# Hybrid stick-breaking / RWKV-7 step on one core: the builder's clock books an in-place operation with its own input, and an eviction nearer to its matmul

## The chip, the cores and the metric

The program runs on one core of a Trainium2 chip. The metric is the device time of one execution in microseconds. Before and after are each the median of several executions; one further execution is recorded by the hardware profiler, and all rows below come from it.

## The reference

One layer of a streaming encoder, for 512 prompt tokens and 8 running streams of 16 tokens (640 tokens, width 1024, 16 heads of 64 in each branch):

```python
h = _rmsnorm(x, norm_g)
proj = jnp.einsum('btd,dc->btc', h, w_in)            # one projection, 10368 columns
# branch A: stick-breaking attention, strictly causal
log_keep = jnp.where(valid, jax.nn.log_sigmoid(-z), 0.0)
later = lax.cumsum(log_keep, axis=3, reverse=True) - log_keep
weight = jnp.where(valid, jnp.exp(jax.nn.log_sigmoid(z) + later), 0.0)
y_a = jnp.einsum('btc,cd->btd', o_a * jax.nn.silu(z_a), w_o_a)
# branch B: RWKV-7, per head a 64x64 state
S = S * w_t - (S kk_t) (kk_t * a_t)^T + v_t k_t^T     # written short
o_t = S r_t
y_b = jnp.einsum('btc,cd->btd', o_b * jax.nn.silu(z_b), w_o_b)
y = jnp.einsum('btd,de->bte', g_a * y_a + g_b * y_b, w_out)
return x + y, k, v, shift_new, wkv_new
```

The final states of the 8 sampled streams (`wkv_sample`) and of the prompt (`wkv_prompt`) are outputs too.

## The kernel before

**Tiling.** Everything is transposed: features lie on the 128 partitions, the 640 tokens on the free axis. A projection job (`gemm_range`) makes 128 output columns for 640 tokens, in two halves of 320. Weights and inputs are each split into a high and a low part, so that for each of 8 slices of the contraction there are three matmuls: `ps_g<-xh,whi`, `ps_g<-xl,whi` and `ps_g<-xh,wlo`, 48 a job. They are the bulk of TensorE's work. After every second slice (six matmuls, below called a piece) the job gives the builder a chance to place something else.

**Stages.** First the norm (up to about 40 us). Then, to about 720 us, the RWKV branch for eight pairs of heads, with projections between. Then a stretch of projections, then attention for eight pairs (about 796 to 1030 us), again with projections between; at last the two branch projections, the merge and the output projection.

**RWKV, per pair of heads.** `prep` makes decay and keys (`wl`, the low part of the two decay and gate matrices, on GpSimd), the operands `H` and `BK` and the masked products `AB`. `prep2` inverts blocks of them through `STG` and `Y`. `chain` walks the chunks of 64 tokens; a step (`step`) goes TensorE `X,H`, ScalarE `RH`, TensorE `RH,AB`, ScalarE `X`, TensorE `X,BKt`, VectorE `X`, and every hand-over passes an engine. `sstate` makes the final states of the sampled streams: GpSimd masks `X` into `ux`, TensorE multiplies it with `BKt` into `psn`, then come three operations in a row:

```python
vtt(sn, psn.rearrange("p (b v) -> p b v", b=8), S0T, ALU.add)
...
gtt(sn, sn, wc[:, 8:16].unsqueeze(2).broadcast_to([128, 8, 64]), ALU.mult)
yield [sn]
```

`vtt` is VectorE, `gtt` is GpSimd, in place; then TensorE transposes `sn` four times. `post` norms and gates the output of a pair; its last part is on GpSimd (`on<-on,V`, `zb<-zb,on`, `zb<-zb,Oa`).

**Attention, per pair.** A sampled block (`KT,qbd`) and eight prompt blocks are each scored on TensorE, pass ScalarE (`kp`, `bt`), GpSimd (`bt<-bt,amsk`) and VectorE (a scan of `kp`, then `bt<-bt,kp`), are transposed on TensorE (`ps_b<-cst,bt`, the flip) and multiplied with the values; `sg` is the gate of the pair's output. `reload("oB")` brings the RWKV branch's output back from memory and splits it over the projections' input tiles: GpSimd copies `xh<-rl`, VectorE makes `xl<-rl,xh`.

**What sets the order.** Each engine runs its instructions in the order in which the program was written, and that order is found while the program is built. The branches are generators, which the `Driver` steps. A `yield [tiles]` says that the stream should go on when these tiles are ready by the builder's clock (`Clock`), an account with one running time for each engine. `Driver.run` compares that with TensorE's time in the account: of the streams that are ready it takes the one of the first priority, and if none is ready it writes a piece of the projection. So what an operation is booked at decides how many projection pieces are written between a hand-over's two ends. `Clock.note` (L138 to L145) books an operation: it starts no sooner than its engine is free and its inputs are ready, and an input that the same engine made counts as ready sooner by `near` (0.25 for TensorE, 0.15 ScalarE, 0.14 VectorE, 0.15 GpSimd), since a result is booked `LAT = 0.25` after its operation's end. `_Eng.__getattr__` (L212 to L217) wraps every instruction: it sorts the operands into inputs and output and calls `note`. All instructions pass its line L213, so rows of the profile are told apart by tile names.

Of the kernel before, what the change touches and what calls it, by code (L numbers as in the profile page):

```python
# [88 lines left out]
class Clock:  # L89
# [46 lines left out]
    def note(self, eng, dur, ins, outs, lat=0.0):  # L136
        st = self.free[eng]
        for i in ins:  # L138
            r = self.ready.get(i)
            if r is not None:  # L140
                st = max(st, r - (self.near[eng] if self.by.get(i) == eng else 0.0))
            if i.startswith("ps_") and self.last.get(i, eng) != eng:
                st = max(st, self.used[i] - 0.12)
        for o in outs:
            st = max(st, self.used.get(o, 0.0) - (self.near[eng] if self.last.get(o) == eng else 0.0))  # L145
        self.free[eng] = st + dur
        if eng == "dma":
            self.wire = max(self.wire, st + dur + lat[1]) + lat[0]
            lat = self.wire + lat[2] - st - dur
        for o in outs:  # L150
            self.ready[o] = st + dur + lat
            self.by[o] = eng
        for o in ins:
            end = st + dur + (lat if eng == "dma" else self.LAT)
            if end > self.used.get(o, 0.0):
                self.used[o], self.last[o] = end, eng
# [5 lines left out]
def _name(ap):  # L162

    if not hasattr(ap, "tensor"):
        return ap
    n = ap.tensor.name
    return f"{n}:{ap.offset % (8 * T) // T}" if n in PARTS else n


def _cols(ap):  # L170
    n = 1
    for d in ap.shape[1:]:
        n *= d
    return n
# [30 lines left out]
class _Eng:  # L205
# [3 lines left out]
    def __getattr__(self, op):  # L209
        f = getattr(self.obj, op)  # L210

        def call(*a, **k):  # L212
            r = f(*a, **k)  # L213
            aps = [x for x in list(a) + list(k.values()) if hasattr(x, "tensor")]
            out = k.get("out", aps[0])
            ins = [x for x in aps if x is not out]
            n = _cols(out)  # L217
            e = self.eng
            lat = Clock.LAT
            if e == "pe":  # L220
                w = k.get("lhsT")
                m, r = (128, 128) if w is None else (_cols(w), w.shape[0])
                if w is None:
                    d = 0.109
                elif w.dtype == F32R:
                    d = max(0.013 + n / 2400.0, 0.107)
                elif w.dtype == F32:
                    d = max(0.026 + n * 0.00087, 0.082 if m > 32 else 0.041) if m <= 64 else \
                        max(n / 600.0 + 0.005, 0.216)
                else:  # L230
                    d = 0.089
                mode = "full" if r > 64 and m > 64 else (r > 32, r > 64, m > 32, m > 64)
                if mode != self.clk.mode:
                    d += 0.1 if self.clk.mode == "full" else 0.2
                    self.clk.mode = mode
            elif e == "act":
                d = 0.065 + n * 0.00085 + 0.1 * sum(hasattr(k.get(x), "tensor") for x in ("scale", "bias"))
                if out.shape[0] < 64:
                    d = 0.12 + n * 0.0021
                elif out.shape[0] < 128:  # L240
                    d += 0.115
                fn = str(k.get("func"))
                t = "sig" if "Sigmoid" in fn or "Tanh" in fn else "exp" if "Exp" in fn else \
                    "sqrt" if "Sqrt" in fn else None
                if t is not None and t != self.clk.tbl:
                    self.clk.tbl = t
                    d += 1.28
            elif e == "dve":
                d = 0.075 + n * 0.00106
                if op == "scalar_tensor_tensor":  # L250
                    d = 0.13 + n * 0.00112
                elif op == "tensor_scalar":
                    d = 0.1 + n * 0.0011 + 0.03 * sum(hasattr(x, "tensor") and _cols(x) == 1
                                                     for x in list(a) + list(k.values()))
                elif op == "tensor_tensor_scan":
                    d = 0.03 + n * 0.0025
                elif op == "reciprocal":
                    d = 0.05 + n * 0.0064
                elif op == "bn_stats":
                    d = 0.126  # L260
                elif op == "transpose" and len(ins[0].shape) > 2 and ins[0].ap[-1][0] > 1:
                    d = 2.03
                if out.shape[0] < 128 and any(_name(x).startswith("ps_") for x in ins if hasattr(x, "tensor")):
                    d += 0.09
            elif e == "pool":
                d = 0.2 + n * (0.0022 if op == "tensor_tensor" else 0.0012)
                if op == "tensor_copy":
                    d = 0.15 + n * 0.0035
            else:
                d = 0.47  # L270
                run = 2.0 if min(x.shape[-1] for x in aps) < 128 else 1.0
                lat = (n * out.shape[0] * 4 * run / 3.6e5, 0.65, 0.93)
            self.clk.note(e, d, [_name(x) for x in ins], [_name(out)], lat)
            return r
        return call
# [1504 lines left out]
```

## Time and profile before

| | us |
|---|---|
| three executions | 1175.71, 1171.71, 1172.51 |
| median | 1172.51 |
| the profiled execution, its own time | 1171.08 |
| span of its trace | 1169.3 |
| TensorE busy (matmul) | 1111.5 |
| VectorE busy | 746.2 |
| ScalarE busy | 629.8 |
| GpSimd busy | 390.5 |

Busy is the time in which at least one instruction of the engine ran. TensorE is busy for 95% of the span, so that 57.8 us are left in which it waits. Its clock can be lower than full (2.4 GHz) in places: the column PEclk of a stretch is the granted share, 0.50 being the level of 1.2 GHz.

### The profile page before, as it was taken

The numbers are of one execution on the slowest core, as the hardware profiler recorded it, in microseconds if no ns is written. First come the engines' busy times: TensorE is split into PE (matmuls) and PEld (weight loads), VectorE is DVE, ScalarE is ACT, GpSimd is POOL, SyncE is SP. The second block draws the span as 40 slices with busy tenths as digits, with TensorE's granted clock in tenths as the row PEclk, the third lists the DMA queues.
The fourth block names the chain that finished last, engine by engine and source line by source line (L and its number), as shares of the span: only waits on it lengthen the run. The fifth ranks groups of instructions, "written<-read, shape, count | busy, mean of one in ns | idle before, by whom it ended". The sixth has DMA issues, their size and how long they took to land. (4 is left out here: it accounts for less than half of the span.)

```text
span 1169.3 us, 25426 instructions
## 1 busy us (share of the span) xinstructions
PE 1111.5 (95%) x10050; PEld 1037.7 (89%) x10050; DVE 746.2 (64%) x1517; ACT 629.8 (54%) x1347; POOL 390.5 (33%) x605
## 2 busy tenths in 40 slices
PE   6999899989999999999899999999999989999997
PEld 4989899979989989889799899998888878899997
DVE  6485974847765867857767544337777688765424
ACT  5636357646666477466575556445555544522223
POOL 3033315125222243342342513034444454323302
PEclk9999999989999999999999999999999999999999
DMA  5222222213132232133132333369666676366312
GB/s 193 78 89 57 78 66 82 84 50 115 62 95 77 67 93 79 55 88 89 52 93 90 98 103 102 108 184 261 180 161 160 172 216 177 82 197 188 105 56 91
DMA packets 205294, 130.70 MB, mean 112 GB/s; under 512 B 78332, under 2 KB 184696, under 8 KB 205176
## 3 DMA queue, kind: packets, MB, share of 16 engines
q1 hardware_dynamic: 204888, 129.03, 37.8%
q8 instruction: 79, 1.29, 0.4%
q14 instruction: 39, 0.32, 0.1%
q0 software_dynamic: 288, 0.05, 0.0%
HBM read 97.70 MB, written 31.35 MB: 110 GB/s over the span
## 5 line engine op out<-in xcount | busy, mean ns | idle before, releaser
L213 PE MATMUL ps_g<-xh,whi 128*128 128x320 f32 (+1 forms) x1424 | 468.5, 329 | 1.7 <-ACT xh L213 1.3
L213 PE MATMUL ps_g<-xl,whi 128*128 128x320 f32 (+1 forms) x1424 | 443.5, 311 | 3.3 <-DVE xl L213 3.3
L213 PE MATMUL ps_g<-xh,wlo 128*128 128x320 f32 (+1 forms) x1424 | 443.0, 311 | 1.4 <-DVE wlo L213 1.4
L213 PEld LDWEIGHTS ps_g<-xh,whi 128*128 128x128 f32 x1424 | 271.4, 191 | 9.3 <-issue 3.0
L213 PEld LDWEIGHTS ps_g<-xl,whi 128*128 128x128 f32 x1424 | 270.9, 190 | 6.4 <-DVE xl L213 4.5
L213 PEld LDWEIGHTS ps_g<-xh,wlo 128*128 128x128 f32 x1424 | 270.0, 190 | 2.4 <-DVE wlo L213 2.4
L213 DVE TENSOR_TENSOR wlo<-raw,whi 128x1024 fp32r<-128x1024 f32 x97 | 123.6, 1274 | 69.6 <-ACT whi L213 69.0
L213 ACT ACTIVATE whi<-raw 128x1024 fp32r<-128x1024 f32 x97 | 102.7, 1059 | 48.6 <-DMA raw<-in_w_o_a_dram 28.6
L213 DVE TENSOR_TENSOR_SCAN kp<-kp,amsk 128x256 f32<-128x256 f32 (+3 forms) x80 | 73.6, 929 | 27.8 <-ACT kp L213 27.7
L213 POOL TENSOR_TENSOR bt<-bt,amsk 128x128 f32<-128x128 f32 x64 | 44.0, 691 | 124.3 <-ACT bt L213 81.5
L213 POOL TENSOR_TENSOR itmp<-INV 128x28 f32<-128x28 f32 (+6 forms) x112 | 47.0, 420 | 90.8 <-DVE INV L213 82.9
L213 ACT ACTIVATE kp<-ps_a 128x512 f32<-128x512 f32 (+3 forms) x72 | 33.1, 460 | 68.0 <-PE ps_a L213 42.2
L213 ACT ACTIVATE RH<-ps_b 128x128 f32<-128x128 f32 (+1 forms) x64 | 19.4, 302 | 77.8 <-PE ps_b L213 77.4
L213 ACT ACTIVATE sp<-ps_g 128x320 f32<-128x320 f32 x80 | 34.6, 437 | 45.9 <-PE ps_g L213 40.6
L213 ACT ACT_TABLE_LOAD x39 | 50.0, 1283 | 8.9 <-DVE BK L213 5.4
L213 DVE SCALAR_TENSOR_TENSOR X<-ps_b,wc,SW 64x64 f32<-64x64 f32 x96 | 26.7, 278 | 35.7 <-PE ps_b L213 34.9
L213 POOL TENSOR_TENSOR on<-on,V 128x640 f32<-128x640 f32 x8 | 12.4, 1550 | 108.9 <-ACT on L213 108.9
L213 DVE TENSOR_TENSOR bt<-bt,kp 128x511 f32<-128x511 f32 (+4 forms) x72 | 42.4, 588 | 7.7 <-POOL bt L213 0.3
L213 POOL TENSOR_TENSOR INV<-INV,itmp 128x28 f32<-128x28 f32 (+6 forms) x112 | 43.6, 390 | 8.8
L213 PE MATMUL ps_b<-cst,bt 128*128 128x128 f32 x192 | 33.5, 278 | 12.4 <-DVE bt L213 11.8
L213 PE MATMUL ps_g<-olo,mgh 128*128 128x256 f32 x160 | 45.0, 281 | 0.0
L213 PE MATMUL ps_g<-ohi,mgh 128*128 128x256 f32 x160 | 45.0, 281 | 0.0
(252 smaller groups left out, 2319.4 us busy)
## 6 DMA issues: line engine op xcount, KB each, us to landing
raw<-in_w_in_dram SPq DMA_DIRECT2D x81, 512.0 KB
q<-dr_q SPq DMA_DIRECT2D x32, 160.0 KB
Kr<-in_cache_sb_k_dram SPq DMA_DIRECT2D x16, 256.0 KB
Vp<-in_cache_sb_v_dram SPq DMA_DIRECT2D x16, 256.0 KB
raw<-in_w_o_b_dram SPq DMA_DIRECT2D x8, 512.0 KB
raw<-in_w_o_a_dram SPq DMA_DIRECT2D x8, 512.0 KB
oraw<-in_w_out_dram SPq DMA_DIRECT2D x4, 1024.0 KB
dr_zB<-zm SPq DMA_DIRECT2D x8, 320.0 KB
```

Of the source, the lines that this page charges most:

```text
L213: r = f(*a, **k)
```

## The change

Two edits of the builder's clock; no instruction of the kernel is written, removed or sized anew.

```diff
@@ -138,7 +138,8 @@
         for i in ins:
             r = self.ready.get(i)
             if r is not None:
-                st = max(st, r - (self.near[eng] if self.by.get(i) == eng else 0.0))
+                by = self.by.get(i)
+                st = max(st, r - (self.near[eng] if by == eng else 0.12 if by == "pe" else 0.0))
             if i.startswith("ps_") and self.last.get(i, eng) != eng:
                 st = max(st, self.used[i] - 0.12)
         for o in outs:
@@ -213,7 +214,7 @@
             r = f(*a, **k)
             aps = [x for x in list(a) + list(k.values()) if hasattr(x, "tensor")]
             out = k.get("out", aps[0])
-            ins = [x for x in aps if x is not out]
+            ins = [x for k, x in enumerate(aps) if x is not out or any(x is y for y in aps[:k])]
             n = _cols(out)
             e = self.eng
             lat = Clock.LAT
```

The first edit: an operation on another engine that reads a result of TensorE is booked 0.12 us sooner. The second: an operand that is the very object given as the output was left out of the inputs before; now its second appearance counts as an input, so that an in-place operation is booked behind the operation that made its operand. It bears on `sn`, on `sg` of attention, on `newton` and on some more.

Both programs hold the same instructions, as many on each engine; their order differs from TensorE's 408th row on, and is the same again in the last 997 rows (the output projection). The helper's line is L214 now, since a line was added above it.

TensorE, the seventh pair's (pair 6) sampled state, from the matmuls on `ux` to the four transposes of `sn` (`ps_g` are projection matmuls, `X,BKt`, `X,AB` and `X,H` are of the chain's steps, `cst,V` and `H,BK` are of `prep`). Before:

```order
L213 MATMUL ps_g<-xh,wlo 128x320
L213 MATMUL ps_b<-X,BKt 128x128
L213 MATMUL ps_c<-X,AB_102 128x128
L213 MATMUL ps_a<-cst,V 128x128 x5
L213 MATMUL ps_g<-xh,whi 128x320
L213 MATMUL ps_g<-xl,whi 128x320
L213 MATMUL ps_g<-xh,wlo 128x320
L213 MATMUL ps_g<-xh,whi 128x320
L213 MATMUL ps_g<-xl,whi 128x320
L213 MATMUL ps_g<-xh,wlo 128x320
L213 MATMUL ps_b<-ux,BKt 64x256 x2
L213 MATMUL ps_b<-cst,sn 128x128 x4
```

The same place now:

```order
L214 MATMUL ps_g<-xh,wlo 128x320
L214 MATMUL ps_b<-ux,BKt 64x256 x2
L214 MATMUL ps_a<-H,BK 128x128 x4
L214 MATMUL ps_g<-xh,whi 128x320
L214 MATMUL ps_g<-xl,whi 128x320
L214 MATMUL ps_g<-xh,wlo 128x320
L214 MATMUL ps_g<-xh,whi 128x320
L214 MATMUL ps_g<-xl,whi 128x320
L214 MATMUL ps_g<-xh,wlo 128x320
L214 MATMUL ps_b<-X,H 128x128
L214 MATMUL ps_c<-X,H 128x128
L214 MATMUL ps_b<-cst,sn 128x128 x4
```

A piece of the projection and some matmuls of `prep` and of the chain now stand between `ux,BKt` and the transposes, where nothing stood.

VectorE, the first pair's `prep2`, from the tile `Y` to `STG` (`H`, `BK` of `prep`; `K`, `shf` are evictions of the projection). Before:

```order
L213 TENSOR_SCALAR Y_1422<-ps_a,half 128x128
L213 TENSOR_TENSOR K<-K,nrm 128x640
L213 SCALAR_TENSOR_TENSOR H<-kkn,E_1176 64x8x64
L213 SCALAR_TENSOR_TENSOR H<-kkn,E_1176 64x2x64
L213 TENSOR_TENSOR BK<-av,sg 64x10x64
L213 TENSOR_TENSOR BK<-K,sg 64x10x64
L213 COPY AB_102<-ps_a 16x8x16 x2
L213 SCALAR_TENSOR_TENSOR STG<-STG,half,ps_a 32x16x8 x2
```

The same place now:

```order
L214 TENSOR_SCALAR Y_1457<-ps_a,half 128x128
L214 SCALAR_TENSOR_TENSOR kkn<-R,prm,K 128x640
L214 SCALAR_TENSOR_TENSOR K<-ps_g,prm,K 128x192
L214 SCALAR_TENSOR_TENSOR K<-ps_g,prm,K 128x8x15
L214 SCALAR_TENSOR_TENSOR K<-ssft,prm,K 128x8
L214 COPY shf<-ps_g 128x9
L214 COPY AB_102<-ps_a 16x8x16 x2
L214 SCALAR_TENSOR_TENSOR STG<-STG,half,ps_a 32x16x8 x2
```

The next pair's `H` and `BK` stood between `Y` and `STG`; they have moved ahead of `Y`, and one long operation and four evictions stand there.

VectorE, the reload of the RWKV output in attention (`xl<-rl,xh`; `kp` and `bt` are the scan and the product of a score block, `ktok`, `ql` and `ks` belong to the next pair's operands). Before:

```order
L213 TENSOR_TENSOR xl<-rl,xh 128x640 x2
L213 COPY ktok<-ps_b 128x512
L213 TENSOR_TENSOR xl<-rl,xh 128x640 x2
L213 TENSOR_TENSOR sg<-ps_c,sg 128x512
L213 COPY ktok<-ps_b 128x128
L213 TENSOR_TENSOR xl<-rl,xh 128x640
L213 TENSOR_TENSOR wlo<-raw,whi 128x1024
L213 TENSOR_TENSOR xl<-rl,xh 128x640 x3
L213 SCALAR_TENSOR_TENSOR kp<-kp,amsk 128x256 x2
L213 TENSOR_TENSOR bt<-bt,kp 128x2x255
```

The same place now:

```order
L214 TENSOR_TENSOR xl<-rl,xh 128x640
L214 SCALAR_TENSOR_TENSOR kp<-kp,amsk 128x256
L214 TENSOR_TENSOR bt<-bt,kp 128x255
L214 TENSOR_TENSOR xl<-rl,xh 128x640
L214 SCALAR_TENSOR_TENSOR kp<-kp,amsk 128x128
L214 TENSOR_TENSOR bt<-bt,kp 128x127
L214 TENSOR_TENSOR ql<-q_11829,qh 128x512 x2
L214 TENSOR_TENSOR xl<-rl,xh 128x640
L214 TENSOR_TENSOR wlo<-raw,whi 128x1024
L214 TENSOR_TENSOR xl<-rl,xh 128x640 x3
```

The reload stood between two pairs' score blocks, behind the last scan of one pair; now its parts lie between a pair's scans.

Counted over TensorE's whole order, 96 projection matmuls fewer stand ahead of the first pair's `KT,qbd` (3381, 3477 before), and 90 of these ahead of the last RWKV pair's output `Oa`. From one pair's `KT,qbd` to the next, and at last to the last flip, there stand 84, 84, 84, 84, 84, 84, 72 and 60, where there stood 84, 84, 96, 96, 96, 90, 78 and 60. Behind the last flip there are 144 more.

## Rows read from the trace of the kernel before

**Rows 1.** The page's first part: the span, busy time by engine.

```profile
span 1169.3 us, 25426 instructions
...
PE 1111.5 (95%) x10050; PEld 1037.7 (89%) x10050; DVE 746.2 (64%) x1517; ACT 629.8 (54%) x1347; POOL 390.5 (33%) x605
```

**Rows 2.** Windows by stage: busy of each engine (instructions), clock, DMA share, GB/s.

```profile
core 0: us, PE busy (x) PEld busy (x) DVE busy (x) ACT busy (x) POOL busy (x), PEclk, DMA share, GB/s
...
40.00:720.00 680.00, 654.28 (x6392) 615.43 (x6392) 457.86 (x1032) 407.45 (x864) 221.43 (x398) 0.99 0.27 80
720.00:800.00 80.00, 80.00 (x575) 78.86 (x575) 26.20 (x66) 39.03 (x86) 15.13 (x14) 1.00 0.58 161
800.00:1040.00 240.00, 224.88 (x2000) 198.61 (x1999) 182.74 (x248) 122.90 (x287) 111.29 (x137) 0.99 0.62 170
```

**Rows 3.** Waits of TensorE: us in total, times, longest us.

```profile
PE ps_b L213 <- DVE bt L213: 11.8, 18, 1.9
PE ps_b L213 <- POOL sn L213: 8.9, 5, 3.9
...
PE ps_a L213 <- DVE STG L213: 4.4, 2, 3.0
PE ps_a L213 <- POOL wl L213: 3.3, 3, 2.7
PE ps_g L213 <- DVE xl L213: 3.3, 5, 1.7
```

**Rows 4.** Timeline, 240.5 to 249.5: start, us, what [idle before <-releaser].

```profile
244.87 0.67 DVE L213 TENSOR_TENSOR sn<-ps_b,S0T 128x512 f32<-128x512 f32 x1
...
245.62 1.04 POOL L213 TENSOR_TENSOR sn<-sn,wc 128x512 f32<-128x512 f32 x1 [3.88 <-DVE sn L213]
...
246.72 1.11 PE L213 MATMUL ps_b<-cst,sn 128*128 128x128 f32 x4 [3.92 <-POOL sn L213]
```

**Rows 5.** Windows, as rows 2: three stretches at the lowered TensorE clock.

```profile
143.00:146.40 3.40, 3.40 (x20) 3.06 (x22) 3.31 (x7) 0.53 (x1) 0.00 (x0) 0.50 0.00 0
245.40:252.30 6.90, 5.58 (x20) 5.19 (x21) 1.64 (x8) 0.60 (x1) 1.14 (x3) 0.51 0.23 38
474.00:477.50 3.50, 3.50 (x22) 3.41 (x17) 3.33 (x15) 0.16 (x1) 0.00 (x0) 0.52 0.41 145
```

**Rows 6.** Timeline, 415 to 424: the sampled state of pair 3.

```profile
418.96 1.54 POOL L213 TENSOR_TENSOR on<-on,V 128x640 f32<-128x640 f32 x1
...
419.06 0.65 PE L213 MATMUL ps_b<-ux,BKt 128*64 128x256 f32 x2 [0.98 <-POOL ux L213]
...
423.17 0.66 PE L213 MATMUL ps_b<-cst,sn 128*128 128x128 f32 x4
```

**Rows 7.** Timeline of TensorE, 141 to 142: the first pair's wait for `STG`.

```profile
141.53 0.68 PE L213 MATMUL ps_a<-STG,AB 32*32 32x32 f32 x10 [2.96 <-DVE STG L213]
```

**Rows 8.** Timeline of TensorE, 577.5 to 581.6: a chain step without cover.

```profile
578.59 0.49 PE L213 MATMUL ps_b<-RH,AB 128*128 128x128 f32 x2
579.69 0.49 PE L213 MATMUL ps_b<-X,BKt 128*128 128x128 f32 x2 [0.61 <-ACT X L213]
```

**Rows 9.** The chain that ended last: one run of projection matmuls.

```profile
857.27 1.76 PE ps_g L213 x12
```

**Rows 10.** Timeline of TensorE: where pairs 0, 2, 4 and 5 of attention begin.

```profile
796.20 0.42 PE L213 MATMUL ps_a<-KT,qbd 128*32 128x128 f32 x8
...
855.02 0.43 PE L213 MATMUL ps_a<-KT,qbd 128*32 128x128 f32 x8
...
914.54 0.43 PE L213 MATMUL ps_a<-KT,qbd 128*32 128x128 f32 x8
...
947.92 0.42 PE L213 MATMUL ps_a<-KT,qbd 128*32 128x128 f32 x8
```

**Rows 11.** Timeline, 932 to 950: the reload on GpSimd and VectorE.

```profile
936.25 7.78 POOL L213 TENSOR_SCALAR xh<-rl 128x640 fp32r<-128x640 f32 x7
...
938.26 2.59 DVE L213 TENSOR_TENSOR xl<-rl,xh 128x640 fp32r<-128x640 f32 x2
...
944.17 0.81 DVE L213 TENSOR_TENSOR xl<-rl,xh 128x640 fp32r<-128x640 f32 x1
```

## The prediction

> **What bounds the kernel now.** I read the page's head first: TensorE is busy for 1111.5 of 1169.3 us, the next engine, VectorE, for 746.2 [rows 1]. The change takes no matmul away, so all that it can win or lose lies in TensorE's 57.8 us of idle time and in stretches at a lowered clock. The windows by stage tell where the idle time is [rows 2]: 25.7 us in the RWKV stage (680.00 less 654.28), none in the stretch of projections behind it, 15.1 us in attention (240.00 less 224.88); the rest is start and end, where the order stays nearly as it was. Then the list of TensorE's waits [rows 3], where the reader is to look for names that the two edits can touch: `sn` (8.9 us in 5 waits), `STG` (4.4), `wl` (3.3), and in attention `bt` (11.8 in 18) and `xl` (3.3).
>
> The second view is the clock. Three stretches of the RWKV stage ran at about 0.5, so at 1.2 GHz: 3.40, 6.90 and 3.50 us [rows 5]. A stretch at 0.50 costs about half its length: 1.7 + 3.4 + 1.7 = 6.8 us. The first lies behind the wait of 2.96 us for `STG` [rows 7], the second around the wait of 3.92 us for `sn` [rows 4]. So a removed stall may give back more than its own length.
>
> **The change part by part.** One projection matmul costs 1.76 / 12 = 0.147 us [rows 9], a piece of six 0.88 us. That is what a stall is filled with.
>
> *sn.* The second edit books the in-place multiplication behind its addition, so the transposes are written later. Before, the addition of pair 1 starts at 244.87, the multiplication at 245.62, and TensorE goes on at 246.72 after 3.92 us [rows 4]. Counted in TensorE's order at such prices, the matmul work between the last `ux,BKt` and the transposes was 2.72, 0.60, 1.19, 2.68, 1.64, 3.21, 0.60, 2.50 us over the eight pairs, and is now 2.26, 3.15, 2.68, 2.42, 7.50, 2.90, 2.43, 3.43 us. What is needed is about 2.3 us where both engines are free (1.85 from the addition's start to the transposes [rows 4], and some 0.5, an estimate by the 0.61 of [rows 8], for the hand-over from TensorE ahead of it), and 4.11 us where GpSimd does `on` (1.54 us) and one `zb` first: 419.06 to 423.17 [rows 6]. In the new order `on` and `zb` stand ahead of `sn` in pairs 2 and 5, which leaves 4.11 - 2.68 and 4.11 - 2.90, together 2.6 us; pairs 0 and others lack some 0.3. So 8.9 becomes 2.9: **-6.0**. Bounds: -8.9 if all is covered, -3 if VectorE is as far behind everywhere as it was in pair 1.
>
> *STG.* The next pair's `H` and `BK` leave the place between `Y` and `STG` in the first pair, so its 2.96 us go [rows 7]; in the second pair the new order puts the same `H` and `BK` and a `wlo` more in that very place, with 3.63 us of TensorE work counted beside them: a new stall that I take a little under the first one, 2.6. 4.4 becomes 2.6: **-1.8** (bounds -4.4 and 0).
>
> *wl.* One piece now stands between `lat,wh` and `lat,wl`, in a wait of 2.7 us [rows 3]: **-0.9**.
>
> *The clock.* The stretch behind pair 1's `sn` stall should go (3.4) and that behind the first `STG` stall (1.7); the third stays, and the new 2.6 us stall gets a stretch of 1.7 with even odds: 6.8 becomes 2.6, **-4.2** (bounds -6.8 and 0).
>
> *The chain.* The first edit books evictions 0.12 us sooner, so consumers are written sooner, with less work between. A hand-over alone is seen in [rows 8]: `RH,AB` at 578.59, `X,BKt` at 579.69, so 1.10 us, of which 0.61 was idle. Counted in the order, the cover of that hand-over falls under 1.10 us in five steps of 64 (0.43, 0.60, 0.76, 0.79, 0.86; before in two, 0.60 and 0.86), that of `Y` in two (0.11, 0.55) and that of `X,H` in one (0.91). The lacks add up to 2.06 - 0.74 + 1.54 + 0.19: **+3.1** (bounds 0, if the missing work is found in matmuls whose records overlap, and +6, if each lacks twice as much).
>
> *Attention.* The starts of `KT,qbd` give the period of a pair [rows 10]. Pairs 0 and 1 took (855.02 - 796.20) / 2 = 29.41 us with 84 projection matmuls each; pairs 2 and 3 (914.54 - 855.02) / 2 = 29.76 us with 96 each. Twelve matmuls more, 1.76 us [rows 9], lengthened the period by 0.35: the period is mostly not set by TensorE's load but by the way of a block through ScalarE, GpSimd, VectorE and back, which is where its `bt` waits come from [rows 3]. The period of the reload, 914.54 to 947.92, took 33.38 us. The new order has 36 matmuls fewer in the periods of 96, 6 fewer in each of two others: 48, or 7.1 us, which run later, behind the last flip, where TensorE is busy anyway. Of these the periods give back 3 x 0.35 + 2 x 0.2 and I allow 0.2 for the reload: 1.6. Net **+5.5** (bounds 0, if the periods follow the load fully, and +7.1).
>
> The sum: -6.0 - 1.8 - 0.9 - 4.2 + 3.1 + 5.5 = -4.3. The profiled execution took 1171.08 us (1.8 beyond its span), so it would take 1166.8; it stands 1.4 under the median of 1172.51, on whose scale that is **1168.2**.
>
> The Trainium skill bears on the reload. The row: two `xl` beside GpSimd's copies took 2.59 us, so 1.30 each, one without a copy beside it 0.81; seven copies took 7.78 us, 1.11 each [rows 11]. The Trainium skill, page "SBUF — State Buffer", section "Who interferes with whom", says that a VectorE instruction with two inputs in SBUF contends with a GpSimd instruction that reads SBUF, and that the shared port pair is held for a whole instruction while the other fully blocks. The row agrees in direction (1.30 against 0.81), though not in a full block, which would add a copy's whole length. By the page alone the reload among the scans would cost what the third rival says; by the rows only the difference, which is the same as before.
>
> **The rivals.**
>
> *Attention keeps pace.* If the smaller load does shorten the periods one for one, +5.5 falls away: 1162.7. For it: TensorE is busy for 224.88 of 240 us there [rows 2], so the slack is small. Against it: 84 and 96 matmuls in nearly one period [rows 10].
>
> *The reload stalls the scans; no change.* `xl` and the copies `xh` now lie among a pair's scans. If each of 8 copies holds VectorE up for its whole 1.11 us, that is 8.9 us; 1.8 of it is in the measured `xl` already; 7.1 us more give 1175.3, which is no change. For it: the slower `xl` beside copies. Against it: 0.49 us each, not 1.11 [rows 11].
>
> *The RWKV stage is as flat as attention; slower.* 90 projection matmuls, 13.2 us, leave the stage ahead of the last pair's `Oa` and run at the end. I took it that the stage shortens by that, stalls apart. If its period is set by the chain of hand-overs, and only a fifth comes out as in attention (0.35 of 1.76), 10.6 us stay: 1178.8. It turns the sign once 8 of the 13.2 us are not given back. For it: it is what attention's periods show next door [rows 10]. Against it: 654.28 of 680.00 us are busy [rows 2], and of the waits that lead the list none is of the chain's own `X` or `RH` [rows 3].
>
> That the edits do nothing is excluded by the order, which differs in all these places.
>
> **How the numbers follow.** No change means within 0.3%, 3.5 us either way. My forecast has 0.45, its own range 1163 to 1172, so about 0.29 faster and 0.16 the same; attention keeping pace 0.20, nearly all faster; the reload 0.20, of it 0.16 the same and 0.04 slower; the flat RWKV stage 0.15, of it 0.13 slower and 0.02 the same. That gives 0.48 faster, 0.35 the same, 0.17 slower. The range reaches below to attention keeping pace with the two rests at zero as well (1162.7 - 2.9 of `sn` - 2.6 of the clock = 1157), above to the flat stage, 1180; some 2 in 10 lie outside.
>
> **What the profile would show.** Right: waits for `sn` near 3 us, in pairs 2 and 5 alone; no lowered clock near the second pair's sampled state; a new wait for `STG` in the second pair; small waits for `X`, `Y` and `AB`; KT,qbd every 29.4 us, and the reload's period near 33. Wrong: a period in attention of 28 or less (the first rival), `bt` waits of over 15 us with `xl` of 2 us (the second), or more idle time in the RWKV stage than its 25.7 us (the third). The weakest steps are attention's +5.5 and the clock's -4.2, since a short stall decides whether a stretch is lowered: among the waits here, one of 2.74 us for `wl` [rows 3] was not followed by such a stretch.

## The result: slower, and the profile after

Twenty executions of the changed kernel took 1174.91 to 1182.6 us, median 1179.74; twenty of the kernel before 1170.74 to 1175.71, median 1172.16. The ratio is 1.0061, 95% interval 1.0049 to 1.0072: 7.6 us slower, where 1168.2 and faster was forecast. The profiled execution of the changed kernel is the lowest of its twenty (1174.91), so its rows understate the loss.

The page's first part and three stages of the changed kernel (the columns of [rows 2]):

```profile
span 1173.1 us, 25419 instructions
...
PE 1112.0 (95%) x10050; PEld 1037.5 (88%) x10050; DVE 752.5 (64%) x1517; ACT 631.1 (54%) x1347; POOL 392.9 (33%) x605
```

```profile
40.00:720.00 680.00, 656.54 (x6437) 617.74 (x6438) 463.44 (x1039) 413.75 (x882) 226.65 (x402) 0.99 0.28 82
720.00:800.00 80.00, 77.43 (x601) 74.43 (x600) 39.03 (x79) 40.59 (x88) 22.14 (x26) 1.00 0.61 173
800.00:1040.00 240.00, 220.98 (x1898) 195.54 (x1898) 172.15 (x231) 115.99 (x265) 102.21 (x121) 0.97 0.59 162
```

TensorE's work is the same 1112 us. What stands out is the clock of attention, 0.97 where it was 0.99. TensorE's waits (us in total, times, longest) answer to [rows 3]:

```profile
PE ps_b L214 <- DVE bt L214: 13.9, 18, 1.9
...
PE ps_a L214 <- DVE H L214: 4.6, 7, 1.0
PE ps_g L214 <- DVE xl L214: 4.5, 6, 1.7
...
PE ps_a L214 <- POOL wl L214: 2.7, 1, 2.7
PE ps_c L214 <- DVE sg L214: 2.3, 5, 1.1
PE ps_a L214 <- DVE Y L214: 2.0, 4, 1.0
...
PE ps_a L214 <- DVE STG L214: 1.2, 1, 1.2
...
PE ps_b L214 <- POOL sn L214: 0.3, 1, 0.3
```

The waits for `sn` are gone (8.9 before); small ones for `H`, `Y` and `sg` have come, and attention's `bt` and `xl` have grown. The starts of the first, the sixth, the seventh and the eighth pair of attention, from TensorE's timeline, answer to [rows 10]:

```profile
776.60 0.42 PE L214 MATMUL ps_a<-KT,qbd 128*32 128x128 f32 x8
...
922.47 0.43 PE L214 MATMUL ps_a<-KT,qbd 128*32 128x128 f32 x8
...
951.67 0.43 PE L214 MATMUL ps_a<-KT,qbd 128*32 128x128 f32 x8
...
989.09 0.42 PE L214 MATMUL ps_a<-KT,qbd 128*32 128x128 f32 x8
```

Five periods take (922.47 - 776.60) / 5 = 29.17 us each, the sixth 29.20; then comes one of 37.42. That is the period with the reload. Two windows of it, from the first copy to the last `xl` and within it the stretch at the lowered clock, then the same first window in the kernel before (row of the trace of before):

```profile
956.42:983.58 27.16, 20.30 (x153) 16.42 (x152) 24.76 (x29) 10.71 (x26) 21.98 (x24) 0.75 0.66 185
966.98:980.63 13.65, 10.02 (x53) 8.23 (x54) 12.65 (x17) 4.53 (x13) 10.79 (x15) 0.50 0.48 146
```

```profile
936.25:948.84 12.59, 9.76 (x71) 7.55 (x71) 12.49 (x15) 3.12 (x8) 8.90 (x9) 0.99 0.59 180
```

The same eight copies and eight subtractions took 12.59 us and now take 27.16, half of it at 1.2 GHz. GpSimd's timeline shows why:

```profile
956.42 2.76 POOL L214 TENSOR_SCALAR xh<-rl 128x640 fp32r<-128x640 f32 x2
959.15 1.35 POOL L214 TENSOR_TENSOR bt<-bt,amsk 128x128 f32<-128x128 f32 x1
960.47 1.84 POOL L214 TENSOR_SCALAR xh<-rl 128x640 fp32r<-128x640 f32 x2
962.28 1.01 POOL L214 TENSOR_TENSOR bt<-bt,amsk 128x128 f32<-128x128 f32 x1
963.27 2.40 POOL L214 TENSOR_SCALAR ks<-kT 64x512 fp32r<-64x512 f32 x2
965.75 1.72 POOL L214 TENSOR_TENSOR sg<-sg,sz 128x640 f32<-128x640 f32 x1
967.44 1.52 POOL L214 TENSOR_TENSOR bt<-bt,amsk 128x128 f32<-128x128 f32 x2
968.93 1.87 POOL L214 TENSOR_SCALAR qh<-q 128x512 fp32r<-128x512 f32 x2
970.77 0.88 POOL L214 TENSOR_SCALAR xh<-rl 128x640 fp32r<-128x640 f32 x1
```

Seven copies stood in a row before [rows 11]. Now the fifth stands behind `ks`, `sg`, two `bt` and `qh`, and starts 8.5 us after the fourth has ended. Until the reload is through, the next projection has no input, so TensorE has few pieces left between the flips, and waits for both, for `xl` and for `bt`.

### The profile page after: what moved, and what is told of

The parts are those of the page before. It is cut to its first block, busy times and chain, and to the rows that moved or that the text cites. A ratio compares the mean times of both kernels' runs of the same rounds, so it can differ in the third digit from the quotient of the medians.

```text
span 1173.1 us, 25419 instructions
## 1 busy us (share of the span) xinstructions
PE 1112.0 (95%) x10050; PEld 1037.5 (88%) x10050; DVE 752.5 (64%) x1517; ACT 631.1 (54%) x1347; POOL 392.9 (33%) x605
## 5 line engine op out<-in xcount | busy, mean ns | idle before, releaser
L214 PE MATMUL ps_g<-xh,whi 128*128 128x320 f32 (+1 forms) x1424 | 465.9, 327 | 0.5 <-ACT xh L214 0.5
L214 PE MATMUL ps_g<-xl,whi 128*128 128x320 f32 (+1 forms) x1424 | 441.8, 310 | 4.6 <-DVE xl L214 4.5
L214 PE MATMUL ps_g<-xh,wlo 128*128 128x320 f32 (+1 forms) x1424 | 440.9, 310 | 0.7 <-DVE wlo L214 0.7
L214 PEld LDWEIGHTS ps_g<-xl,whi 128*128 128x128 f32 x1424 | 269.1, 189 | 8.8 <-DVE xl L214 6.7
L214 PEld LDWEIGHTS ps_g<-xh,whi 128*128 128x128 f32 x1424 | 269.6, 189 | 7.5 <-issue 2.3
L214 PEld LDWEIGHTS ps_g<-xh,wlo 128*128 128x128 f32 x1424 | 268.4, 188 | 1.3 <-DVE wlo L214 1.3
L214 DVE TENSOR_TENSOR wlo<-raw,whi 128x1024 fp32r<-128x1024 f32 x97 | 127.1, 1310 | 62.5 <-ACT whi L214 61.6
L214 ACT ACTIVATE whi<-raw 128x1024 fp32r<-128x1024 f32 x97 | 102.5, 1057 | 65.2 <-PE ps_g L214 47.4
L214 DVE TENSOR_TENSOR_SCAN kp<-kp,amsk 128x256 f32<-128x256 f32 (+3 forms) x80 | 74.5, 939 | 35.6 <-ACT kp L214 35.4
L214 POOL TENSOR_TENSOR bt<-bt,amsk 128x128 f32<-128x128 f32 x64 | 47.8, 751 | 127.6 <-ACT bt L214 97.8
L214 POOL TENSOR_TENSOR itmp<-INV 128x28 f32<-128x28 f32 (+6 forms) x112 | 43.7, 390 | 83.8 <-DVE INV L214 76.1
L214 ACT ACTIVATE kp<-ps_a 128x512 f32<-128x512 f32 (+3 forms) x72 | 33.1, 460 | 67.8 <-PE ps_a L214 37.5
L214 ACT ACTIVATE sp<-ps_g 128x320 f32<-128x320 f32 x80 | 34.9, 438 | 60.4 <-PE ps_g L214 51.7
L214 ACT ACTIVATE RH<-ps_b 128x128 f32<-128x128 f32 (+1 forms) x64 | 19.3, 302 | 67.4 <-PE ps_b L214 67.1
L214 POOL TENSOR_TENSOR on<-on,V 128x640 f32<-128x640 f32 x8 | 12.4, 1552 | 125.2 <-ACT on L214 125.2
L214 DVE SCALAR_TENSOR_TENSOR X<-ps_b,wc,SW 64x64 f32<-64x64 f32 x96 | 26.7, 278 | 36.3 <-PE ps_b L214 35.4
L214 PE MATMUL ps_b<-cst,bt 128*128 128x128 f32 x192 | 34.2, 283 | 15.2 <-DVE bt L214 13.9
L214 DVE TENSOR_TENSOR bt<-bt,kp 128x511 f32<-128x511 f32 (+4 forms) x72 | 43.1, 598 | 8.2 <-POOL bt L214 0.6
L214 POOL TENSOR_TENSOR INV<-INV,itmp 128x28 f32<-128x28 f32 (+6 forms) x112 | 43.2, 386 | 8.8
L214 PE MATMUL ps_g<-olo,mgh 128*128 128x256 f32 x160 | 45.0, 281 | 0.0
L214 PE MATMUL ps_g<-ohi,mgh 128*128 128x256 f32 x160 | 45.0, 281 | 0.0
```

## The experiments

Every execution is listed with its span and mean granted clock. Span times clock is the **time at full clock**; the rest of the span is the **lost clock**, half of all that runs at 1.2 GHz. Both are means over a kernel's executions (before: the 87 beside the experiments). "Scans" are VectorE's `kp` scans between the first and the last `xl` of the reload, and "left" the projection matmuls behind the last flip, both counted in the order. Each ratio is to the kernel before as it ran beside that kernel: its medians were 1173.17 us (beside `e1_only` and `e2_only`), 1173.22 (`after_fill` to `e2_act`), 1172.28 (`after_edge` to `e2_act_edge`) and 1172.70 (the last three rows). Differences of medians across these groups are good to about 1 us.

| kernel | median us (n) | ratio to before, 95% | full clock | lost | scans | left |
|---|---|---|---|---|---|---|
| before | 1172.16 (20) | | 1155.8 | 15.2 | 0 | 1002 |
| changed | 1179.74 (20) | 1.0049 to 1.0072 | 1157.6 | 20.1 | 5 | 1146 |
| e1_only | 1181.79 (6) | 1.0053 to 1.0094 | 1162.3 | 17.1 | 5 | 1062 |
| e2_only | 1174.81 (12) | 1.0001 to 1.0033 | 1153.4 | 19.6 | 5 | 960 |
| after_fill | 1179.11 (7) | 1.0032 to 1.0066 | 1161.7 | 15.3 | 5 | 1146 |
| after_act | 1175.26 (12) | 1.0002 to 1.0029 | 1155.2 | 18.3 | 3 | 1128 |
| before_mid | 1182.28 (6) | 1.0055 to 1.0095 | 1158.1 | 22.2 | 5 | 960 |
| e2_act | 1165.18 (6) | 0.9911 to 0.9949 | 1147.3 | 16.1 | 3 | 936 |
| after_edge | 1166.00 (10) | 0.9933 to 0.9966 | 1150.5 | 13.5 | 0 | 1086 |
| after_late | 1176.65 (8) | 1.0028 to 1.0061 | 1156.0 | 19.0 | 5 | 1062 |
| before_act | 1170.30 (12) | 0.9967 to 1.0001 | 1154.5 | 13.6 | 0 | 984 |
| e2_act_edge | 1168.73 (12) | 0.9964 to 0.9992 | 1149.0 | 18.2 | 0 | 876 |
| e1_edge | 1172.24 (12) | 0.9984 to 1.0015 | 1157.3 | 13.5 | 0 | 1002 |
| e2_edge | 1177.44 (12) | 1.0022 to 1.0051 | 1155.8 | 19.6 | 0 | 900 |
| after_edge_act | 1163.08 (5) | 0.9891 to 0.9932 | 1148.2 | 12.5 | 0 | 1068 |

**A second look, and each edit alone.** `after_again` is the changed kernel unaltered; `e1_only` and `e2_only` leave out the other edit's line.

> The changed kernel unaltered, a second look. Clock theory (the two edits leave the time at full clock as it was, and what is lost is lost to stretches at 1.2 GHz, which fall in other places from one execution to the next): span times granted clock within 1155 to 1159 us as in both profiles so far (1169.3 x 0.99 and 1173.1 x 0.986), the span anywhere from 1173 to 1181, with lowered stretches in attention. Order theory (attention and the end lose by the projections that were moved out, the clock is incidental): the same places lowered as in the first profile, span near 1173, and any longer span with a longer time at full clock.

> The first edit alone (results of TensorE booked 0.12 us sooner; an in-place operand not booked). Four of eight sampled states have no projection piece between ux and the transposes of sn again. Clock theory: sn waits back at 7 to 10 us, a lowered stretch behind the longest of them, slower than before by 3 to 10 us with span times clock 2 to 5 above that of before. Order theory (what counts is how many projections are left for attention: 3447 ahead of the first KT,qbd, against 3477 and 3381): between before and after, 1174 to 1177.

> The second edit alone. Every sampled state has 12 to 24 projection matmuls or 12 to 16 others between ux and the transposes, and 3537 projection matmuls stand ahead of the first KT,qbd (60 more than before). Clock theory: sn waits under 3 us, no lowered stretch behind a sampled state, 4 to 10 us faster than before (1162 to 1168). Order theory: faster as well by the sn waits (6 us), but attention has fewer pieces than before (its seven full periods 84 to 90), so that 1 to 3 us of it are lost: 1167 to 1170.

The second look took 1176.95 us, span times clock 1156.4, within the clock theory's range. In the RWKV stage its stretches lie elsewhere, and two others lie in the reload, which was lowered in the first profile too (windows of `after_again`):

```profile
137.09:143.92 6.83, 6.76 (x116) 6.65 (x117) 3.95 (x10) 3.85 (x7) 0.00 (x0) 0.50 0.19 55
229.25:232.66 3.41, 3.41 (x20) 3.19 (x22) 0.78 (x2) 0.79 (x2) 3.31 (x3) 0.50 0.02 5
969.94:973.36 3.42, 3.42 (x24) 3.09 (x25) 3.18 (x5) 1.36 (x5) 3.42 (x4) 0.50 0.68 222
976.77:983.60 6.83, 5.45 (x27) 4.08 (x26) 6.62 (x10) 1.38 (x5) 3.79 (x6) 0.50 0.38 112
```

The first edit alone was 8.6 us slower than the kernel before beside it. That is past the order theory's range and within the clock theory's 3 to 10, but it comes from the time at full clock (6.5 above before, 2 to 5 expected) more than from lost clock (1.9): half a miss for the clock theory too. The second alone wins 2.4 at full clock and loses 4.4 of clock: a miss for both. In the table both have the reload among five scans, as the changed kernel has, and the kernel before has none. So a new theory: it is the reload's place that costs. (What the second edit does by `sn` alone is not shown by any run: the orders of `e2_only` and of before part at 76.7 us, where the first addition of `sn` starts at 162.0, so other in-place operations move things too.)

**Filling the reload, moving its copies, moving it.** `after_fill` writes dummy matmuls where TensorE waits. They share a bank with the first branch projection's sums, so that this projection's first half is not the reference's; all else has its size and place.

```diff
...
+            if (p, it) == (6, ("p", 2, 0)):
+                fill(ps, 16)
...
+                        if i == nbx + 1 and half == 0 and q == 1:
+                            fill(ps, {2: 18, 3: 12, 5: 10}.get(k, 0))
```

`after_act`, `e2_act` (on the second edit alone) and later `before_act` move the copies of this reload:

```diff
-                    gcopy(hi[:, p, :], ts[p])
+                    if n == "oB":
+                        act(out=hi[:, p, :], in_=ts[p], func=AF.Copy)
+                    else:
+                        gcopy(hi[:, p, :], ts[p])
```

`before_mid` holds attention back until a count of projection pieces, which shifts the reload against the pairs:

```diff
+    pieces = [0]
...
+                        pieces[0] += 1
...
+        if not p:
+            yield lambda: pieces[0] >= 584
```

> The changed kernel with 56 dummy matmuls (128x128 in bf16, results never read) on TensorE at four places of the reload where it waits in both profiles: 16 ahead of one flip of the seventh pair, 18, 12 and 10 ahead of the third, fourth and sixth xl matmul. No other engine's order changes. Reload theory (TensorE starves in the reload, since it lies among the seventh pair's scans, and the clock falls there): the stretch of 10 to 14 us at 1.2 GHz in the reload shrinks to 3.4 or nothing, the lost clock (span times one less the granted clock) falls from 20 us to about 15, the time by 3 to 6 us to 1174 to 1177. Spread theory (the clock is lost to many small waits all over, the reload's place is incidental): 1180 as before, or up to 4 us slower by the dummy work.

> The changed kernel, the reload's eight copies xh<-rl on ScalarE instead of GpSimd; TensorE's order up to attention is the same. Reload theory: GpSimd's bt products and VectorE's xl no longer queue behind and beside the copies, the waits for xl (4.5 us) halve, the lowered stretch of the reload shrinks, 4 to 8 us faster than the changed kernel: 1172 to 1176. Spread theory: the reload's engines have slack enough, within 2 us of 1179.7.

> The kernel before, attention's first pair held until 584 pieces (3504 projection matmuls) are written, 54 matmuls more than it waits for by itself. The reload then falls among the fifth pair's scans (five scans between its first and last xl, as in the changed kernel, none before), and 42 projection matmuls fewer are left behind the last flip. Reload theory: a lowered stretch of 10 to 17 us in the reload against 3.4, lost clock up by 3 to 5 us; against it the full-clock time falls by up to 4.5 (42 matmuls moved from the end into attention, at the prices of the prediction); 1171 to 1175 with lost clock near 20. Spread theory: lost clock stays near 15.7, 1168 to 1170.

> The second edit alone, with the reload's eight copies on ScalarE. Reload theory: lost clock from 19.6 to 15 us or less, waits for xl halved, 1166 to 1170, faster than the kernel before (1172.8). Spread theory: 1173 to 1176, as the second edit alone (1174.8).

With the filling, the reload keeps one short stretch (window of `after_fill`):

```profile
978.79:982.21 3.42, 3.42 (x22) 2.72 (x21) 3.31 (x6) 0.78 (x3) 1.08 (x2) 0.50 0.34 100
```

Its lost clock falls by 4.8 us, as the reload theory has it, but the time does not, and stays by the spread theory's 1180: the dummy work costs 4.1 at full clock. `before_mid` moves the reload of the kernel before in among five scans: 9.1 us slower than before beside it, with 22.2 us of lost clock against 15.2; I expected less, since I had counted on a gain of 4.5 at full clock, and it lost 2.3. The copies on ScalarE win 4.5 us on the changed kernel (5.5 by the ratios to before) and 9.6 on the second edit alone. All four go the reload theory's way in lost clock, three by other sizes in time. But how the copies on ScalarE win is not what that theory said: TensorE's waits for `xl` were to halve, and rose, from 4.5 us to 6.2 (`after_act`) and from 4.6 to 6.7 (`e2_act`). Fewer scans lie within the reload there, three for five; the rest stays open.

**Twins.** `after_edge` and `after_late` are the changed kernel held until 566 and 569 pieces, three pieces apart; TensorE's order is the same up to attention. What follows differs a little besides (the last column of the table). In one the reload falls between two pairs, in the other among five scans.

> The changed kernel, attention's first pair held until 566 pieces are written (42 projection matmuls more ahead of it). The reload then falls between the sixth pair's last scan and the seventh's first, none among it. Reload theory (the place of the reload among the scans starves TensorE and lowers its clock): the reload's lowered stretch is 3.4 us or none, lost clock (span times one less the granted clock) near 16 us instead of 20, 1173 to 1177. Spread theory (the place is incidental): lost clock near 20, within 2 us of its twin with 569 pieces.

> The twin: held until 569 pieces, 18 matmuls later than the one with 566. The reload falls among the sixth pair's scans again, five of them within it. Reload theory: a lowered stretch of 10 to 17 us there, lost clock near 20 us or more, 3 to 6 us slower than its twin: 1178 to 1182. Spread theory: the same time as the twin within 2 us.

> The kernel before with the reload's eight copies on ScalarE; its reload lies between two pairs already. Reload theory: little to win there, 1170 to 1174, lost clock as before (16). Spread theory (GpSimd's load in attention is what counts, wherever the reload lies): as much as the second edit alone won by it, 6 to 10 us, 1163 to 1167.

> The second edit alone with the copies on ScalarE and attention's first pair held until 590 pieces (30 matmuls more), so that the reload lies between two pairs. Reload theory: the stretch of 6.8 us in the reload falls to 3.4 or none and its wait for xl with it, 1161 to 1165. Spread theory: 1165 as without the hold, within 2 us.

The reload's windows of `after_edge`, then of `after_late` with its two stretches:

```profile
947.54:960.13 12.59, 9.77 (x75) 7.66 (x79) 12.48 (x15) 3.11 (x8) 8.60 (x9) 1.00 0.58 178
```

```profile
939.14:966.30 27.16, 19.61 (x148) 15.76 (x148) 24.77 (x29) 10.81 (x26) 21.98 (x24) 0.79 0.66 190
951.32:954.73 3.41, 3.38 (x20) 2.70 (x14) 3.17 (x5) 1.83 (x6) 3.41 (x5) 0.50 0.60 188
958.14:968.38 10.24, 8.64 (x43) 6.88 (x44) 8.68 (x13) 1.83 (x6) 3.25 (x4) 0.50 0.41 126
```

These are the numbers of before and of the changed kernel over again: 12.59 and 27.16 us. TensorE is idle for 2.82 us in the one (12.59 - 9.77) and 7.55 in the other, 4.7 more; in the 13.65 us at 1.2 GHz it is busy for 12.02, which costs 6.0. Together that is an estimate of 10.7 us, where the medians differ by 10.65 (5.5 at full clock, 5.4 lost). So the reload is enough to account for the whole difference. Both twins came out below their ranges (1173 to 1177 and 1178 to 1182) and further apart than the 3 to 6 us expected. `after_edge` is 6.3 us faster than before beside it. `before_act` won 2.0 us, with an interval (0.9967 to 1.0001) that includes no change, as expected: at the edge there is little to relieve. `e2_act_edge` missed: slower than without the hold, though its reload is at the edge. Its waits say that another place ran dry:

```profile
PE ps_g L213 <- DVE oAl L213: 3.7, 3, 2.8
PE ps_g L213 <- POOL oAh L213: 3.4, 1, 3.4
```

`oAh` and `oAl` are the second reload, of attention's output, behind the last flip. With 876 matmuls left there, of which 864 are the oA projection itself and what follows, 12 are left to cover it.

**One edit at a time, at the edge.** `e1_edge` holds until 582 pieces, `e2_edge` until 594, `after_edge_act` is `after_edge` with the copies on ScalarE.

> The first edit alone, attention's first pair held until 582 pieces, so that the reload lies between two pairs as in the kernel before (no scan within it, 1002 projection matmuls behind the last flip, as before). What differs from the kernel before is then the RWKV stage: the sn stalls stay (5.6 us against 8.9) and the chain is booked tighter. If the first edit costs by itself (+3.1 us of chain in the prediction): 1173 to 1177. If it costs nothing and the whole loss of the first edit alone (1181.8) was the reload's place: 1168 to 1172.

> The second edit alone, held until 594 pieces, the reload between two pairs (no scan within it), 900 projection matmuls behind the last flip against 960 without the hold. If the reload's place costs the second edit what it cost the twins of the changed kernel (10.6 us): 1162 to 1167, faster than the kernel before by the sn stalls and their clock alone. If it costs less where 20 projection halves fewer wait behind the last flip: 1168 to 1173.

> The changed kernel with 566 pieces and the reload's copies on ScalarE as well. If the copies on GpSimd cost only where they lie among the scans: within 2 us of the 1166.0 without that. If they cost beside the next pair's operands too: 1162 to 1164, the fastest of all.

With the reload at the edge the first edit alone is level with before (1172.24, between its two ranges), and 9.6 us faster than with the reload among the scans. `e2_edge` missed, in part for the reason of `e2_act_edge`: 900 matmuls are left, 36 of them to cover the second reload, and it starves (its waits, and the clock there):

```profile
PE ps_g L213 <- POOL oAh L213: 2.4, 1, 2.4
PE ps_g L213 <- DVE oAl L213: 2.1, 3, 1.2
```

```profile
1047.31:1057.55 10.24, 6.82 (x20) 5.25 (x21) 5.59 (x6) 1.06 (x1) 4.76 (x5) 0.50 0.94 326
```

The waits for `oAh` and `oAl` follow what is left: 7.1 us with 876, 4.5 with 900, and none of TensorE's in the profiles with 936 or more. But in `e2_edge` the first reload is late as well, though no scan lies within it: a copy waits 1.09 us for its data and another 0.89, the reload takes from 910.49 to 926.20 us, TensorE's longest wait for `xl` is one of 3.08, and a stretch of 6.83 us at 1.2 GHz (921.01 to 927.84) goes with it. So an edge without scans is not always a place without cost.

```profile
924.05 0.63 PE L213 MATMUL ps_g<-xl,whi 128*128 128x320 f32 x1 [3.08 <-DVE xl L213]
```

So the second edit alone, with both reloads covered, stays unmeasured; on top of the first it is worth 1172.24 - 1166.00 = 6.2 us, in two kernels that also differ in what is left (1002 and 1086). `after_edge_act` is the fastest of all, 9.6 us under the kernel before beside it, and lies in the range for copies that cost beside the next pair's operands too.

## Why the prediction was wrong, step by step

**The step that failed** is attention's: "I allow 0.2 for the reload". The order at this place was seen, and its price was put at nothing, with 0.2 us even counted as given back. Between the twins the place is worth 10.6 us, 9.6 between `e1_edge` and `e1_only`, 9.1 between before and `before_mid`, each time with the same change of place. In the two profiles the reload's period took 33.38 us with 96 projection matmuls [rows 10] and takes 37.42 with 72: 4.0 longer, with 3.5 us of matmuls less in it, together 7.6.

**That the rest of the sum nearly holds is luck in part.** Less the twins' 10.65 us the changed kernel would stand at 1169.1, an estimate, where 1168.2 was forecast. (`after_edge` itself, 1166.0, also has 60 matmuls fewer behind the last flip.) But two misses cancel in that. The last flip starts, before and now:

```profile
1026.99 0.27 PE L213 MATMUL ps_b<-cst,bt 128*128 128x128 f32 x1
```

```profile
1010.52 0.27 PE L214 MATMUL ps_b<-cst,bt 128*128 128x128 f32 x1
```

Attention took 230.79 us from the first `KT,qbd` on [rows 10] and takes 233.92, with 48 matmuls (7.0 us) fewer: a loss of 10.2 where 5.5 was forecast, of which 7.6 lie in the reload's period and only 2.6 elsewhere. Up to the first `KT,qbd` 5.5 us are won beyond the matmuls that moved, where 9.8 were forecast; behind the last flip 0.9. So in these two profiles, 3.8 us apart where the forecast had -4.3, the RWKV stage misses by about as much as attention. Its idle time fell by 2.3 us (25.7 to 23.5), where the waits were to give 5.6; the clock won 3.4 of its 4.2 in this profile, and nothing on average (below).

**The signs.** None of the forecast's signs of being wrong came: the periods without the reload are 29.17 us on average (the sign was 28 or less), the `bt` waits 13.9 (over 15), an `xl` 1.0 (2), the RWKV stage's idle time 23.5 (over 25.7). What told was one of the signs of being right, the reload's period "near 33".

**The rival "the reload stalls the scans" had the place, not the reason.** It let each copy hold up VectorE, 7.1 us and no change. But an `xl` takes no longer among the scans (VectorE's group of `after_late`: its busy us and mean ns stand behind the first bar) than at the edge (1006 ns in `after_edge`, 1072 before):

```profile
L214 DVE TENSOR_TENSOR xl<-rl,xh 128x640 fp32r<-128x640 f32 x8 | 7.8, 1009 | 0.0
```

With the copies on ScalarE it takes 851 (`after_act`) and 815 (`before_act`), so a copy on GpSimd beside it costs some 0.2 us. The Trainium skill, "SBUF — State Buffer", section "Summary: rules for kernel authors", has the second of two such instructions to issue block fully until the first finishes; these rows show that one slows the other, but by far less than a whole copy's 1.1 us. What costs is, by GpSimd's timeline above, the order in the queues: copies and subtractions wait their turn behind score blocks, score blocks behind them, and the projection that would cover both has no input.

**The clock, -4.2.** Not won. The stall of pair 1 and its stretch are gone. But over seven profiles with the changed kernel's order up to attention (itself, `after_again`, `after_fill`, `after_act`, `after_edge`, `after_late`, `after_edge_act`) the RWKV stage had 6.8 to 17.1 us at 1.2 GHz, on average 13.7, and with the order of before it had 13.7 in each of three (itself, `before_mid`, `before_act`; [rows 5] add up to 13.8 by their wider windows). New stretches lie behind the smaller waits for `STG`, `Y` and `H`, and about 229 us. And the clock of the reload, priced at nothing, cost 6.8 us in the first profile and 5.1 in the second look, where the kernel before lost 1.7 in a stretch of 3.41 at the reload's end (948.58), which [rows 5] do not have: 3.4 to 5.1 more. Together the lost clock rose by 4.9 us.

**sn, -6.0.** Right, and better: 0.3 us of wait are left, not 2.9; pairs 2 and 5, for which 2.6 us were counted, hardly wait.

**STG, wl, chain.** `STG` 1.2 us instead of 2.6, but in the first pair (at 132.88), not in the second, where none came, and with 2.0 for `Y` beside it. `wl` -0.6 instead of -0.9, by luck: the wait of 2.74 that was meant is 2.67 long still, with nothing written between `lat,wh` and `lat,wl` there; two small ones of 0.3 went. `X`, `RH` and `AB` rise by 2.3 us of the 3.1 forecast. Not foreseen: `H` from 1.7 to 4.6, which `prep`'s matmuls wait for, and `s0r`, which comes from memory, from 0.8 to 2.8. In all, the first `KT,qbd` comes 19.6 us sooner (796.20 [rows 10] against 776.60), 14.1 of them the 96 matmuls that moved: 5.5 won where -6.0 - 1.8 - 0.9 - 4.2 + 3.1 has 9.8. Three more profiles with the same order up to there (`after_again`, `after_fill`, `after_act`) begin attention at 777.76, 778.46 and 780.50, and so won 4.3, 3.6 and 1.6. The rival of the flat RWKV stage is out even so: what was moved out came out. (By its own sum its sign turns once 4.3 us are not given back; 8 is where it is slower by more than 0.3%.)

**The flat periods of attention.** Right between 78 and 96 matmuls a pair: 29.17 us with 84, 29.4 forecast. That what is moved behind the last flip is only a loss is wrong: it covers the second reload, and in the two kernels with 876 and 900 left it is missing.

**The first edit** costs nothing that can be measured by itself (`e1_edge`, 0.9984 to 1.0015), where the chain was to cost 3.1; its waits for `sn` are 3.3 us shorter there (5.6 against 8.9), so it loses some of that elsewhere.

## What to carry to other kernels

Where a builder's account sets the order, a small edit shifts everything behind it, and what decides can be where a distant, rare block lands: follow such blocks (here the reloads, on whose end TensorE's filler work depends) through both orders before pricing the stalls that the edit is meant for. Two in-order queues that interleave a block with latency-bound work make the block and the work late together; hold the block to a gap, or give it an engine with time to spare. For a place to hold, a shift of three pieces was worth 10 us; so try several, look at the reload's window in each, and see that the next such block is still covered.

## What the runs showed of the hardware

The level of 1.2 GHz came without a long idle time ahead of it: in the changed kernel TensorE was busy for 10.02 of the 13.65 us in the reload, and the longest of its waits in the 8 us before was 1.63 us. Nor does one wait always bring it: the wait of 2.7 us for `wl` at 77 us was followed by a stretch at 80.75 us in `after_edge` and at 80.92 in `after_late`, by none in the changed kernel, whose order is the same there. So one order gave different stretches from one execution to the next: granted clocks of 0.979 to 0.987 in twenty executions of the changed kernel, a lost clock of 15.3 to 24.8 us, where the time at full clock ran from 1154.1 to 1159.8. So a change's time at full clock and its lost clock are better told apart: the two moved in opposite directions in `e2_only` and in `after_fill`.
